# A grouped softmax streamed through one core: one broadcast multiply per tile in place of eight scalings, and tiles of 128 rows instead of 256

## The chip, the cores and the metric

The kernel runs on one core of a Trainium2 chip. A core has several engines that run side by side and meet only through semaphores. Four of them matter here. VectorE (DVE in the profile) reduces and does elementwise work. ScalarE (ACT) evaluates functions such as the exponential. SyncE (SP) has no arithmetic; it issues transfers. Sixteen DMA engines, shared by all, move data between the device memory (HBM) and the on-chip memory (SBUF), which has 128 partitions. The metric is the device time of one execution in microseconds (us); lower is better.

## The reference

The input is a tensor of 4 x 4096 rows of 4352 f32 numbers. Each row is cut into 8 groups of 544, and each group becomes a softmax of its own.

```python
def setup_inputs():
    B, N, D, G = 4, 4096, 4352, 8
    return {"x": np.random.randn(B, N, D).astype(np.float32)}

def reference(x):
    B, N, D = x.shape
    G = 8
    Dg = D // G
    x_g = x.reshape(B, N, G, Dg)
    x_g = x_g - x_g.max(axis=-1, keepdims=True)
    exp = np.exp(x_g)
    out = exp / exp.sum(axis=-1, keepdims=True)
    return out.reshape(B, N, D).astype(np.float32)
```

In all, 285 MB are read and 285 MB are written.

## The kernel before

The 16,384 rows are cut into 64 tiles of 256 rows. A tile puts two adjacent rows into each of the 128 partitions (`R = 2`), which makes 34,816 consecutive bytes per partition, in HBM as in SBUF. There are six buffers (`NBUF = 6`), and everything is done in place in a buffer: the tile is loaded into it, turned into exponentials, scaled, and stored from it.

A tile has two units of work, one for each of its two rows per partition. A unit is 128 rows, and it has two steps:

- `expo` (lines 55 to 69): VectorE takes the negated maximum of each of the 8 groups (line 58, one instruction over 128 x 4352 elements). ScalarE then does 8 activations (line 62), one for each group: each one takes exp(x - max) in place and sums its 544 results on the way. The profile shows each sum being read out as an instruction of its own.
- `scale` (lines 71 to 77): VectorE takes the reciprocals of the 8 sums (line 74), then does 8 multiplications (line 76), one for each group, each by one number per partition.

The order is written out by hand; no planner moves anything. Units are staggered by one: the loop emits `expo` of unit n and then `scale` of unit n-1. On VectorE this gives: maximum of unit n, reciprocals and scalings of unit n-1, maximum of unit n+1, and so on. ScalarE works on unit n while VectorE scales unit n-1.

All transfers are issued by SP on one queue, and the 16 DMA engines take them in the order of issue. At the start, `AHEAD = NBUF - 1`, so 5, loads are issued. After that, when the last unit of tile i has been scaled, SP issues the store of tile i (line 50) and then the load of tile i+5 (line 47). That load goes into the buffer of tile i-1, so it has to wait until the store of tile i-1 has landed. SP works strictly in order, so while a load waits there, the store of the next tile stands behind it.

Of the kernel before, what the change touches and what calls it, by code (L numbers as in the profile page):

```python
# [1 line left out]

# [4 lines left out]


@with_exitstack
def kernel(  # L10
    ctx: ExitStack,
    tc: tile.TileContext,
    x: bass.AP,
    out: bass.AP,
):
    nc = tc.nc
    G = 8
    P = 128
    R = 2
    NBUF = 6  # L20
    xf = x.flatten_outer_dims()
    of = out.flatten_outer_dims()
    N, D = xf.shape
    Dg = D // G
    f32 = mybir.dt.float32

    pool = ctx.enter_context(tc.tile_pool(name="io", bufs=NBUF))
    small = ctx.enter_context(tc.tile_pool(name="small", bufs=4))

    spans = []  # L30
    at = 0
    while at < N:
        r = min(R, (N - at) // P)
        spans.append((at, r))
        at += r * P
    nt = len(spans)
    tiles = {}
    sums = {}

    def rows(dram, i):  # L40
        at, r = spans[i]
        return dram[at:at + r * P].rearrange("(p r) d -> p (r d)", r=r)

    def load(i):
        xt = pool.tile([P, R * D], f32, name="xt")
        tiles[i] = xt
        nc.sync.dma_start(out=xt[:, :spans[i][1] * D], in_=rows(xf, i))  # L47

    def store(i):
        nc.sync.dma_start(out=rows(of, i), in_=tiles[i][:, :spans[i][1] * D])  # L50

    def row(i, r):
        return tiles[i][:, r * D:(r + 1) * D].rearrange("p (g d) -> p g d", g=G)

    def expo(i, r):
        xr = row(i, r)
        mx = small.tile([P, G], f32, name="mx")
        nc.vector.reduce_max(out=mx, in_=xr, axis=mybir.AxisListType.X, negate=True)  # L58
        sm = small.tile([P, G], f32, name="sm")
        sums[i, r] = sm  # L60
        for g in range(G):
            nc.scalar.activation(  # L62
                out=xr[:, g, :],
                in_=xr[:, g, :],
                func=mybir.ActivationFunctionType.Exp,
                bias=mx[:, g:g + 1],
                scale=1.0,
                accum_out=sm[:, g:g + 1],
            )

    def scale(i, r):
        xr = row(i, r)
        rs = small.tile([P, G], f32, name="rs")
        nc.vector.reciprocal(out=rs, in_=sums.pop((i, r)))  # L74
        for g in range(G):
            nc.vector.tensor_scalar_mul(  # L76
                out=xr[:, g, :], in0=xr[:, g, :], scalar1=rs[:, g:g + 1])

    AHEAD = NBUF - 1
    work = [(i, r) for i in range(nt) for r in range(spans[i][1])]
    with tc.manual_schedule():
        for i in range(AHEAD):
            load(i)
        for n in range(len(work) + 1):
            if n < len(work):
                expo(*work[n])
            if n:
                i, r = work[n - 1]  # L90
                scale(i, r)
                if r == spans[i][1] - 1:
                    store(i)
                    if i + AHEAD < nt:
                        load(i + AHEAD)


# [1 line left out]
_INS = ['x']  # L99
_OUTS = [((4, 4096, 4352), 'float32')]  # L100


# [23 lines left out]
```

## Time and profile before

| | |
|---|---|
| time, median of 3 runs | 1335.33 us (1334.61 to 1335.8) |
| profiled execution, its own time | 1335.33 us |
| span of that execution, first to last instruction | 1333.5 us |
| VectorE busy | 1041.7 us (78%), 1280 instructions |
| ScalarE busy | 764.4 us (57%), 2049 instructions |
| DMA engines busy with the kernel's queue | 99.3% of 16 engines' span |
| moved over the span | 428 GB/s, reads and writes together |

"Span" runs from the first to the last instruction of the profiled execution; what lies around it is in the execution's own time. A group of instructions is shown with its line in the kernel, its engine, its operation, what it writes and reads, how many there were, then busy time and mean duration in ns, and after the second bar the idle time of the engine just before these instructions with what ended most of it. "SPq" is SP's queue of DMA issues. For DMA issues the last number is the median time from issue to landing. Waiting of an engine that isn't the slowest costs nothing in itself.

### The profile page before, as it was taken

What the parts mean: (1) busy time and instruction counts of PE and PEld (TensorE: products, weight loads), DVE (VectorE), ACT (ScalarE), POOL (GpSimd) and SP (SyncE); (2) the same over time, 40 slices, a digit from 0 to 9 for tenths busy, and PEclk for the clock granted to TensorE, in tenths of its full rate; (3) what the DMA queues carried; (4) which work ended last, traced back from release to release, by engine and by line L of the source; (5) the groups of instructions that cost most, each with busy time, mean ns of one, the idle gap of its engine ahead of it and who ended that gap; (6) DMA issues with size and microseconds to landing.
All of it is one profiled execution on the core that took longest, in us unless ns stands there. A gap on an engine that the chain in (4) does not pass through costs nothing.

```text
span 1333.5 us, 3809 instructions
## 1 busy us (share of the span) xinstructions
DVE 1041.7 (78%) x1280; ACT 764.4 (57%) x2049; POOL 0.2 (0%) x4
## 2 busy tenths in 40 slices
DVE  5999887787877878778778787787877878778771
ACT  4777665555655556555565565655656556555560
POOL 0000000000000000000000000000000000000000
DMA  9999999999999999999999999999999999999996
GB/s 403 428 423 432 432 432 431 433 432 431 432 432 434 434 432 434 430 434 434 434 431 433 434 434 434 431 432 435 432 434 432 431 434 434 433 435 433 433 433 283
DMA packets 18460, 570.66 MB, mean 428 GB/s; under 512 B 2048, under 2 KB 2048, under 8 KB 2048
## 3 DMA queue, kind: packets, MB, share of 16 engines
q1 hardware_dynamic: 18432, 570.43, 99.3%
q14 instruction: 28, 0.23, 0.0%
HBM read 285.21 MB, written 285.21 MB: 428 GB/s over the span
## 4 chain that ended last, share of the span: by engine, by line
DMA 92%; DVE 4%; ACT 1%; SPq 1%; issue 0%; DVEq 0%; ACTq 0%
DMA out_dram<-xt 89%; DMA xt<-in_x_dram 3%; DVE mx L58 2%; DVE xt L76 1%; ACT xt L62 1%; SPq L47 1%; DVE rs L74 0%; DVEq L121 0%; ACTq L121 0%; ACTq L62 0%; SPq L50 0%
## 5 line engine op out<-in xcount | busy, mean ns | idle before, releaser
L62 ACT ACTIVATE xt<-xt,mx 128x544 f32<-128x544 f32 x1024 | 751.3, 735 | 522.0 <-DVE mx L58 504.4
L58 DVE TENSOR_REDUCE mx<-xt 128x8 f32<-128x4352 f32 x128 | 599.3, 4683 | 253.5 <-DMA xt<-in_x_dram 253.5
L76 DVE TENSOR_SCALAR xt<-xt,rs 128x544 f32<-128x544 f32 x1024 | 434.3, 499 | 4.5
L62 ACT ACTIVATION_READ_ACCUMULATOR xt<-xt,mx 128x1 f32 x1024 | 191.4, 187 | 0.0
L74 DVE RECIPROCAL rs<-sm 128x8 f32<-128x8 f32 x128 | 24.9, 194 | 4.0 <-ACT xt L62 4.0
L62 ACT ACT_TABLE_LOAD x1 | 1.3, 1283 | 13.7 <-DMA xt<-in_x_dram 13.7
L110 POOL MEMSET const-bfloat16-1.0<- 128x1 bf16 x1 | 0.1, 101 | 0.0
L110 POOL MEMSET const-uint8-127<- 128x1 uint8 x1 | 0.1, 101 | 0.0
L110 POOL MEMSET const-float32-0.0<- 128x1 f32 x1 | 0.1, 98 | 0.2 <-issue 0.2
L110 POOL MEMSET const-float32-1.0<- 128x1 f32 x1 | 0.1, 98 | 0.0
## 6 DMA issues: line engine op xcount, KB each, us to landing
xt<-in_x_dram SPq DMA_DIRECT2D x64, 4352.0 KB, 30.8
out_dram<-xt SPq DMA_DIRECT2D x64, 4352.0 KB, 40.7
```

What stands on the lines that cost most here:

```text
L47: nc.sync.dma_start(out=xt[:, :spans[i][1] * D], in_=rows(xf, i))
L58: nc.vector.reduce_max(out=mx, in_=xr, axis=mybir.AxisListType.X, negate=True)
L62: nc.scalar.activation(out=xr[:, g, :], in_=xr[:, g, :], func=mybir.ActivationFunctionType.Exp, bias=mx[:, g:g + 1], scale=1.0, accum_out= ...
L74: nc.vector.reciprocal(out=rs, in_=sums.pop((i, r)))
L76: nc.vector.tensor_scalar_mul(out=xr[:, g, :], in0=xr[:, g, :], scalar1=rs[:, g:g + 1])
L110: nc = _bacc.Bacc("TRN2", target_bir_lowering=False, num_devices=1)
```

## The change

Three things change together. A tile has 128 rows, one per partition (`R = 1`), so a transfer is half as large (17,408 bytes per partition), there are 128 tiles, and each tile is one unit of work. There are 12 buffers instead of 6; they take the same room. Loads run `NBUF - 2`, so 10, tiles ahead, and the load of tile i+10 goes into the buffer of tile i-2. And the 8 scalings of a unit become one multiplication of the 128 x 4352 unit by the reciprocals, in which each of the 8 numbers of a partition is repeated along its group by a step of zero.

```diff
@@ -16,8 +16,8 @@
     nc = tc.nc
     G = 8
     P = 128
-    R = 2
-    NBUF = 6
+    R = 1
+    NBUF = 12
...
@@ -72,13 +72,12 @@
         xr = row(i, r)
         rs = small.tile([P, G], f32, name="rs")
         nc.vector.reciprocal(out=rs, in_=sums.pop((i, r)))
-        for g in range(G):
-            nc.vector.tensor_scalar_mul(
-                out=xr[:, g, :], in0=xr[:, g, :], scalar1=rs[:, g:g + 1])
+        nc.vector.tensor_mul(
+            out=xr, in0=xr, in1=rs.unsqueeze(2).to_broadcast([P, G, Dg]))
...
-    AHEAD = NBUF - 1
+    AHEAD = NBUF - 2
```

## The prediction

> **What bounds the kernel now.** I read the page first, then the waits of the DMA-issuing queue, then that queue's issues in order of time, and last the stretches around the end. The page, parts 1, 3, 5 and 6:
>
> ```profile
> span 1333.5 us, 3809 instructions
> DVE 1041.7 (78%) x1280; ACT 764.4 (57%) x2049; POOL 0.2 (0%) x4
> ...
> q1 hardware_dynamic: 18432, 570.43, 99.3%
> ...
> L58 DVE TENSOR_REDUCE mx<-xt 128x8 f32<-128x4352 f32 x128 | 599.3, 4683 | 253.5 <-DMA xt<-in_x_dram 253.5
> L76 DVE TENSOR_SCALAR xt<-xt,rs 128x544 f32<-128x544 f32 x1024 | 434.3, 499 | 4.5
> ...
> L74 DVE RECIPROCAL rs<-sm 128x8 f32<-128x8 f32 x128 | 24.9, 194 | 4.0 <-ACT xt L62 4.0
> ...
> xt<-in_x_dram SPq DMA_DIRECT2D x64, 4352.0 KB, 30.8
> out_dram<-xt SPq DMA_DIRECT2D x64, 4352.0 KB, 40.7
> ```
>
> The 16 DMA engines work for 99.3% of the span. VectorE works for 78% and its largest idle time, 253.5 us, waits for a load. ScalarE waits for VectorE. So transfers set the pace. The queue that issues them waits too, for a buffer to be emptied:
>
> ```profile
> SPq L47 <- DMA out_dram<-xt: 1145.0, 58, 20.7
> ```
>
> That wait costs nothing while transfers are still queued. The issues near the end, in order of time, show the pace:
>
> ```profile
> 1167.27 0.33 SPq L47 DMA_DIRECT2D xt<-in_x_dram  x1
> ...
> 1188.74 0.33 SPq L47 DMA_DIRECT2D xt<-in_x_dram  x1
> ...
> 1209.31 0.33 SPq L47 DMA_DIRECT2D xt<-in_x_dram  x1
> ...
> 1229.89 0.33 SPq L47 DMA_DIRECT2D xt<-in_x_dram  x1
> ...
> 1250.45 0.33 SPq L47 DMA_DIRECT2D xt<-in_x_dram  x1
> ```
>
> A tile of 256 rows (one load and one store) takes 20.57 us, so a transfer takes 10.28; a load lands after 30.8, three transfers, a store after 40.7, four. Every sixth tile takes 0.9 us more (here 21.47). Last, the stretches at the end (busy time of VectorE, ScalarE and GpSimd, clock, DMA share, GB/s):
>
> ```profile
> 1305.00:1310.00 5.00, 0.00 (x0) 0.00 (x0) 0.00 (x0) 1.00 1.00 432
> ...
> 1320.00:1325.00 5.00, 0.00 (x0) 0.00 (x0) 0.00 (x0) 1.00 0.29 125
> 1325.00:1330.00 5.00, 0.00 (x0) 0.00 (x0) 0.00 (x0) 1.00 0.13 56
> ```
>
> Arithmetic is over by 1304 and the transfers still run at full rate for 15 us. Then most engines are done, and a share of 0.13 means that two of 16 go on to the end. The time is that of the slowest DMA engine, some 12 us behind the others.
>
> **The change part by part.** The profiled execution took 1335.33 us, 1.83 more than its span, and is itself the median of the three runs, so sums go straight against 1335.33.
>
> *VectorE.* Removed: 1024 scalings, 434.3 us. Added: 128 multiplies of 128x4352. The trace of before has no such instruction. Lower bound: the eight scalings as they stand, 3.39 us in a row. Upper bound: two operands read one after the other at the reduce's rate, 2 x 4.68 = 9.37. I take 4.68, the row of the reduce, which also goes once over 4352 f32 elements. That adds 128 x (4.68 - 3.39) = 165 us of VectorE work. A row's turn on VectorE is now 8.13 us (scalings start at 24.61, 32.74 and 40.87), of which 4.74 is not scaling; it becomes 4.74 + 4.68 = 9.42, while the transfers give a row 10.28. All 165 us lie beside transfers: cost 0. The cover ends at a multiply of 10.28 - 4.74 = 5.54 us; above it every 0.1 us costs 12.8.
>
> A rule speaks against this edit: the Trainium skill, "VectorE: DVE Perf Modes", section "The perf-mode tier table", has f32 tensor_scalar at two elements a cycle and tensor_tensor at one. The scaling row agrees with the first half (544 elements in 499 ns); no row here shows the second. Its section on the TRN2 errata gives (N+151)/0.96 ns for an f32 tensor_tensor, which for 4352 elements I estimate at 4.69 us: were VectorE the bound, +166 us; under the transfers, nothing.
>
> *Queue depth.* Loads go 10 tiles ahead in 12 buffers, so load i+10 waits for store i-2 instead of load i+5 for store i-1. When that store lands, four transfers of 5.14 us are still queued (loads i+8 and i+9, stores i-1 and i), 20.6 us; before, two of 10.28 (load i+4, store i), 20.6 too. What stands behind the waiting load on SP's queue is store i+1, and it is later than its data in both. In the steady part a tile's data lands 5.14 us after the landing on which I count, its row is scaled some 20 us later (its reduce 4.7, its exponentials 6.0, its turn behind the next reduce, the multiply), and the store's turn on SP comes seven tiles on, at 72 us. Nothing starves: cost 0.
>
> *Start.* The first load is half as long, so it lands near 8.5 us instead of 13.65, and store n is ready near 24 + 9.4n. SP first blocks at load 12, which waits for store 0, landing near 59; store 3 is ready at 52. The ten prefetched loads keep the engines busy to 54. An earlier start of arithmetic buys nothing, as DMA starts at 0.73 in both.
>
> *End.* The last load has five transfers to land (26 us) and its row needs some 20 more, but the last store comes to its turn behind about 13 transfers (67 us). The shorter last store is hidden as the longer one was: 0.
>
> *SP's issues.* 128 more at 0.33 to 0.46 us are some 50 us more on a queue that waited 1145: 0.
>
> *Transfers twice as many, half as long.* This is the part on the path. Each of 16 engines moves eight packets of 34,816 bytes per transfer now (16,384 in 128 transfers); it will move eight of 17,408 in each of 256. The trace's records of single packets, which no view lists, give 1,288 ns for 34,816 bytes and 309 ns for an instruction packet of 8,192. The difference, 979 ns for 26,624 bytes, is 36.77 ns per 1,000 bytes; eight packets at that rate are 10.24 us. The pace was 10.28. So about 0.04 us per transfer is not bytes (ends of packets, the semaphore write). 128 more of these: +5.0 us. Lower bound 0, if those 0.04 us are bytes after all. Upper bound: the same two records leave 1,288 - 1,280 = 8 ns per packet, 1,024 more packets per engine are 8.2, and 128 semaphore packets of 9 ns are 1.2: +9.4. I take 5.0, because the measured pace is shorter than eight whole records (10.30), so their ends overlap.
>
> The Trainium skill, "DMA: Bandwidth & Descriptors", section "Anatomy of one DMA", puts a fixed 2.0 us on each DMA: as a serial cost I estimate +256 us for 128 more. The pace speaks otherwise: 10.28 leaves room for 0.04, not 2, since further transfers stand queued.
>
> *Instruction fetches.* The packet records show an instruction packet ahead of each of the long tiles, about 124 us apart, on the engine that ends last; I read them as VectorE's, since six tiles are some 128 of its instructions. With 384 instead of 1280 compute instructions most of them go. But a second engine has its own, about 72 us apart (ScalarE's count fits), 0.62 us each, and ends only 0.4 us earlier. What is late next is therefore that one: -0.4 us, not -8.
>
> *Where loads and stores first meet.* Between 50 and 100 us the rate dips (page, second and third slice 428 and 423 against 433 later); smaller transfers could lengthen or shorten that, by less than 2 us either way: 0.
>
> Sum: 1335.33 + 5.0 - 0.4 = 1339.9.
>
> **The rivals.**
> 1. *Rate by bytes alone.* The 0.04 us is not per transfer: 1335 to 1337.9. For it: it is a difference of two near numbers, and the instruction packet goes to another memory. Against: a semaphore packet per engine and transfer is in the records.
> 2. *Faster: the fetch penalty shrinks with the packets.* A fetch takes 309 ns, but the data packet after it is also some 310 ns longer. If that second part follows the packet's size and falls away, ScalarE's 16 fetches cost 5 us less: 1335.33 - 0.4 - 5 + 5 = 1335 with my transfer cost, 1330 without it. It decides once the gain passes the transfer cost by 2.7. Nothing in the trace separates the two parts by size.
> 3. *Transfers get worse than their fixed cost.* Smaller pieces of memory turn by turn, with the packets of 1.4 to 2.2 us that the records show in the first 325 us lasting on. One more percent of the pace is 13 us: 1345 to 1360. Against: these packets vanish later on in before.
> 4. *VectorE becomes the bound.* A multiply over 5.54 us: at 6.0, 1335 + 59 = 1394; at 9.37, some 1825. Against: the reduce at 4.68 with the same element count.
>
> **How the numbers follow.** Forecast (1338.0 to 1344.5) 0.52; rate by bytes 0.25; faster 0.10; worse transfers 0.08; VectorE 0.05. The range 1333.5 to 1346 leaves out most of the faster case, most of the worse one and VectorE's, about 0.2. A measurement of this kernel tells 0.2%, 2.7 us, from no change: below 1332.7 faster, 0.10; between, 0.25; above 1338.0 slower, 0.65. The likeliest case's own range is 1338 to 1344.5.
>
> **What would show it.** Loads issued 10.32 us apart, not 10.28; DMA share still 99%; multiplies near 4.7 us and VectorE near 1225 us busy (599 + 25 + 128 x 4.69), 91% of the span; a load landing near 26 us and a store near 31; the rare long tiles at spacings that belong to ScalarE alone; the last engine again some 12 us behind. The prediction is wrong if a pace under 10.30 appears, if VectorE's idle time before the reduce goes to nothing, or if the engines end together.

## The result and the profile after

The changed kernel takes 1341.01 us (median of 4 runs, 1339.41 to 1341.88), the kernel before 1335.57 beside it (4 runs, 1334.61 to 1336.1). The ratio is 1.004, with a 95% interval of 1.0023 to 1.0058: slower by 0.4%. The forecast was 1339.9.

The profiled execution of the changed kernel took 1339.41 us, the least of its four; its span is 1337.6 against 1333.5. The lines of its page that answer to those of before:

```profile
span 1337.6 us, 3339 instructions
...
DVE 1210.8 (91%) x384; ACT 764.3 (57%) x2049; POOL 0.2 (0%) x4
...
q1 hardware_dynamic: 36864, 570.44, 99.6%
...
L58 DVE TENSOR_REDUCE mx<-xt 128x8 f32<-128x4352 f32 x128 | 599.6, 4684 | 83.7 <-DMA xt<-in_x_dram 83.7
L75 DVE TENSOR_TENSOR xt<-xt,rs 128x4352 f32<-128x4352 f32 x128 | 600.6, 4692 | 4.4
...
xt<-in_x_dram SPq DMA_DIRECT2D x128, 2176.0 KB, 25.8
out_dram<-xt SPq DMA_DIRECT2D x128, 2176.0 KB, 30.6
```

VectorE took on 169 us of work, and all of it came out of its idle time before the reduce (253.5 us before, 83.7 now). The transfers stayed the bound, at 99.6%. A load lands after five transfers, a store after six. The issues of SP's queue in the middle of the span show the pace, and one of the long tiles that remain (665.55 to 676.50):

```profile
634.57 0.33 SPq L47 DMA_DIRECT2D xt<-in_x_dram  x1
...
644.87 0.33 SPq L47 DMA_DIRECT2D xt<-in_x_dram  x1
...
655.25 0.33 SPq L47 DMA_DIRECT2D xt<-in_x_dram  x1
...
665.55 0.33 SPq L47 DMA_DIRECT2D xt<-in_x_dram  x1
...
676.50 0.33 SPq L47 DMA_DIRECT2D xt<-in_x_dram  x1
```

A tile of 128 rows takes 10.33 us (10.30, 10.38, 10.30), where half a tile of before took 10.28. Two stretches, as busy time of VectorE, ScalarE and GpSimd, clock, DMA share and GB/s, show the middle and the end. The kernel before:

```profile
600.00:900.00 300.00, 238.27 (x291) 172.92 (x464) 0.00 (x0) 1.00 1.00 433
```

The changed kernel:

```profile
600.00:900.00 300.00, 273.61 (x87) 172.90 (x464) 0.00 (x0) 1.00 1.01 431
...
1325.00:1330.00 5.00, 0.00 (x0) 0.00 (x0) 0.00 (x0) 1.00 0.31 132
1330.00:1335.00 5.00, 0.00 (x0) 0.00 (x0) 0.00 (x0) 1.00 0.09 38
```

The rate is down from 433 to 431 GB/s, and the end still belongs to one or two of the 16 DMA engines (a share of 0.09 is 1.4 of them).

A finer pace comes from the trace's records of landings, which no view lists: each transfer has 16, one per DMA engine. The first of the 16, followed from transfer to transfer over the last two thirds of the span, gives the pace of an engine that nothing disturbs; the distance from the first to the last is how late the last engine is. "Pace" and "lateness" below mean these two.

### The profile page after: what moved, and what is told of

It reads as the page before. It is cut to its first block, busy times and chain, and to the rows that moved or that the text cites. A ratio compares the mean times of both kernels' runs of the same rounds, so it can differ in the third digit from the quotient of the medians.

```text
span 1337.6 us, 3339 instructions
## 1 busy us (share of the span) xinstructions
DVE 1210.8 (91%) x384; ACT 764.3 (57%) x2049; POOL 0.2 (0%) x4
## 3 DMA queue, kind: packets, MB, share of 16 engines
q1 hardware_dynamic: 36864, 570.44, 99.6%
## 4 chain that ended last, share of the span: by engine, by line
DMA 83%; DVE 11%; issue 2%; ACT 1%; SPq 1%; ACTq 0%
DMA out_dram<-xt 80%; DVE xt L75 6%; DVE mx L58 5%; DMA xt<-in_x_dram 3%; ACT xt L62 1%; SPq L47 1%; DVE rs L74 0%; SPq L50 0%; ACTq L120 0%
## 5 line engine op out<-in xcount | busy, mean ns | idle before, releaser
L58 DVE TENSOR_REDUCE mx<-xt 128x8 f32<-128x4352 f32 x128 | 599.6, 4684 | 83.7 <-DMA xt<-in_x_dram 83.7
L75 DVE TENSOR_TENSOR xt<-xt,rs 128x4352 f32<-128x4352 f32 x128 | 600.6, 4692 | 4.4
```

What stands on the lines that cost most here:

```text
L75: nc.vector.tensor_mul(out=xr, in0=xr, in1=rs.unsqueeze(2).to_broadcast([P, G, Dg]))
```

## The experiments

Two accounts stood against each other at first: the transfers (twice as many, each with a fixed cost) and VectorE (165 us more work that is perhaps not quite covered).

### The multiply alone

```diff
 # kernel before, R = 2, NBUF = 6, AHEAD = 5
-        for g in range(G):
-            nc.vector.tensor_scalar_mul(...)
+        nc.vector.tensor_mul(
+            out=xr, in0=xr, in1=rs.unsqueeze(2).to_broadcast([P, G, Dg]))
```

> The kernel before with only the scalings replaced by the broadcast multiply; tiles stay at 256 rows. Transfer theory (the 5 us come from twice as many transfers, VectorE's extra work is covered): no slower than before, 1335.57 - 0.4 = about 1335, loads still 20.57 us apart, multiply 4.69 us, VectorE near 1210 us busy. VectorE theory (the longer multiply is what costs): about 1341, the time of the changed kernel.

Measured: 1335.49 us, ratio to before 0.9994 (0.9983 to 1.0005). The page of this kernel:

```profile
DVE 1207.3 (91%) x384; ACT 764.4 (57%) x2049; POOL 0.2 (0%) x4
```

VectorE is as busy as in the changed kernel, and nothing is lost against the 1335.75 of the kernel before beside it. The pace of the transfers is 10.283 us, that of before.

### The tiles alone

```diff
 # changed kernel, R = 1, NBUF = 12, AHEAD = 10
-        nc.vector.tensor_mul(...)
+        for g in range(G):
+            nc.vector.tensor_scalar_mul(
+                out=xr[:, g, :], in0=xr[:, g, :], scalar1=rs[:, g:g + 1])
```

> The changed kernel with the eight scalings put back; tiles of 128 rows, 12 buffers, 10 ahead. Transfer theory: as slow as the changed kernel, 1341, a little more (up to 0.7) if VectorE's fetches make its DMA engine the last again; pairs of transfers 10.33 us apart. VectorE theory: back to 1335.6.

Measured: 1341.78 us, ratio 1.0041 (1.0029 to 1.0053). VectorE is back to 1046.8 us (78%), and the loss is all there. With the run before, this settles it: the loss comes with the smaller transfers, and the multiply, in this place, costs nothing.

### More packets in as many transfers, and more transfers still

The first kernel keeps the 128 transfers but takes each partition's two rows from places 128 rows apart, so a partition's part is two pieces of 17,408 bytes:

```diff
 # kernel before; the tile's side of load and store is split in the same way
-        return dram[at:at + r * P].rearrange("(p r) d -> p (r d)", r=r)
+        return dram[at:at + r * P].rearrange("(r p) d -> p r d", r=r)
```

> The kernel before, but the two rows of a partition come from row p and row p+128 of the tile, so each partition's part is two pieces of 17,408 bytes: 128 transfers as before, twice the packets. If the cost sits with the packets: the pace of a transfer goes from 10.283 to near 10.32 and the time to 1339 to 1341. If it sits with the transfer (semaphore, issue): pace 10.283 and 1335.6.

The second cuts each transfer of the changed kernel into two halves of its columns:

```diff
 # changed kernel; store likewise
+        for h in range(0, D, D // 2):
+            nc.sync.dma_start(out=xt[:, h:h + D // 2], in_=rows(xf, i)[:, h:h + D // 2])
```

> The changed kernel with every transfer cut once more, into two of 8,704 bytes per partition: 512 transfers. Transfer theory, the measured 0.0436 us for each of 128 added ones, now 256 more: 1341 + 11 = 1352, DMA share still 99%. Rate by bytes alone (the 5 us came from something else in the change): 1341.

Measured: 1339.13 us (ratio 1.002, 1.0011 to 1.0029) and 1350.55 (1.0107, 1.0092 to 1.0122). The four kernels in order, per 4.456 MB (one transfer of before, or as many of the others as make that up):

| kernel | data packets per engine | semaphore packets per engine | pace, us |
|---|---|---|---|
| before | 8 | 1 | 10.283 |
| same transfers, split packets | 16 | 1 | 10.321 |
| changed kernel | 16 | 2 | 10.327 |
| half rows | 32 | 4 | 10.414 |

The first two differ by eight packets: 37.5 ns, 4.7 ns for each. The second and third differ by one semaphore packet: 6.1 ns. The fourth was not used for this, and these two sizes give it: 10.327 + 16 x 0.0047 + 2 x 0.0061 = 10.414. So, by the pace, the cost sits mostly with the packets and a little with the transfers. The medians say it more roughly: against the 1335.75 of the kernel before beside them, the split packets cost 3.4 us and the half rows 14.8, where 128 times the difference in pace is 4.8 and 16.7. What is left of 10.283 without them is 10.240 us, 435.2 GB/s.

The rate in the middle of the half-row kernel, in the same columns as above:

```profile
600.00:900.00 300.00, 270.93 (x86) 169.54 (x456) 0.00 (x0) 1.00 1.01 428
```

Its share stands at 1.01 and only 428 GB/s go through: engines that never rest and move less. The page of a kernel at a full DMA share doesn't show this cost as idle time; it shows it as GB/s.

### Larger transfers

```diff
 # kernel before, with the broadcast multiply
-    R = 2
-    NBUF = 6
+    R = 3
+    NBUF = 4
```

> The kernel before with tiles of 384 rows, three rows and 52,224 bytes per partition, 4 buffers, loads 3 ahead, and the broadcast multiply: 43 tiles, 86 transfers instead of 128. Transfer theory: 42 transfers fewer at 0.0436 us is 1.8 us less, and 0.4 less by VectorE's fetches, 1333.3. Against it: a start or an end that the larger tiles leave uncovered, 1336 or more.

Measured: 1340.14 us, ratio 1.0027 (1.0017 to 1.0038): slower, the case written against the theory. Its GB/s in 40 slices:

```profile
GB/s 414 361 400 441 430 428 436 430 427 441 428 434 431 430 434 438 430 436 431 430 445 425 430 443 427 437 436 428 436 435 430 439 430 430 445 425 436 438 388 338
```

The gain is there in the steady part: 15.403 us per transfer between 400 and 1200 us, and the sizes above give 1.5 x 10.240 + 8 x 0.0047 + 0.0061 = 15.403. But three loads of 15.4 us are used up before the first tile of three rows is ready, and the second and third slices drop to 361 and 400. In the records of landings 8.0 us are lost by 100 us, against 1.4 in the kernel before: 6.6 more, which the 1.8 gained don't pay for. A cover that the smaller tiles have is gone at the start.

### The last engine: fewer instructions, and more

To test what makes the last engine late, one kernel takes the maximum and its subtraction out of the computation, and with them most instructions:

```diff
 # kernel before, with the broadcast multiply
-        nc.vector.reduce_max(out=mx, in_=xr, axis=mybir.AxisListType.X, negate=True)
-        for g in range(G):
-            nc.scalar.activation(... bias=mx[:, g:g + 1], accum_out=sm[:, g:g + 1])
+        nc.scalar.activation(out=xr, in_=xr, func=mybir.ActivationFunctionType.Exp)
...
+        nc.vector.reduce_sum(out=sm, in_=xr, axis=mybir.AxisListType.X)
```

> The kernel before without the maximum and its subtraction (left out of the computation): one activation over a whole row of 8 groups, then the sums by VectorE, the reciprocals and the broadcast multiply. Same transfers, ScalarE 128 activations instead of 1024 with 1024 reads. Fetch theory: nearly no fetches, the last engine's 12 us shrink to 2 or 3, about 1326. If the lateness of the last engine has another cause: 1335.

Measured: 1329.12 us, ratio 0.9949 (0.9937 to 0.996). Its page, and the end:

```profile
DVE 1218.4 (92%) x384; ACT 484.4 (36%) x129; POOL 0.2 (0%) x4
...
q14 instruction: 6, 0.05, 0.0%
```

```profile
1320.00:1325.00 5.00, 0.00 (x0) 0.00 (x0) 0.00 (x0) 1.00 0.23 97
1325.00:1330.00 5.00, 0.00 (x0) 0.00 (x0) 0.00 (x0) 1.00 0.01 3
```

The packets of the kind "instruction" are what is called fetches here. With 6 of them in place of 28, the pace is 10.283, that of before, and the lateness at the end is 6.0 us instead of 12.2. So half of the lateness is left nearly without fetches; the expectation of 2 or 3 us was too small. The landing records of the kernel before show the other half directly: up to 330 us the lateness comes to 6.0, and from there to 12.3 it rises in seven steps of 0.94 to 1.02 us, each 4 to 7 us after an instruction packet of the series that stands some 124 us apart. What makes the 6 us that fetches don't explain (3.2 of them are there by 140 us in this run) stays open.

Sixteen tiny activations more per row were to double ScalarE's fetches:

```diff
 # kernel before, after the 8 activations of a row
+        for k in range(16):
+            nc.scalar.activation(
+                out=junk[:, :1], in_=mx[:, :1],
+                func=mybir.ActivationFunctionType.Exp, bias=mx[:, 0:1], scale=1.0)
```

> The kernel before with 16 tiny activations of one column more in each row's work on ScalarE, results unused: ScalarE's instructions nearly double, its work stays under the pace of the transfers. Fetch theory (the last DMA engine is late by instruction fetches, 0.62 us each): 16 more fetches, about 10 us more, 1345, and the stretch with few engines at the end about 22 us long. If fetches don't set the end: 1335.6.

Measured: 1431.54 us, ratio 1.0713 (1.07 to 1.0727). This says nothing on fetches:

```profile
DVE 1048.2 (73%) x1280; ACT 1338.9 (94%) x4097; POOL 0.2 (0%) x4
...
L72 ACT ACTIVATE junk<-mx 128x1 f32<-128x1 f32 x2048 | 600.7, 293 | 62.6
```

An activation of one column takes 293 ns, and ScalarE became the bound. With 8 instead of 16 it does not:

```diff
-        for k in range(16):
+        for k in range(8):
```

> As the run with 16 extra activations in each row, but 8: that run made ScalarE the bound (94% busy, 293 ns each), so it said nothing on fetches. With 8, a row takes ScalarE 6.0 + 8 x 0.32 = 8.6 us, under the 10.28 of the transfers. Fetch theory: half as many ScalarE instructions again, 8 fetches more at 0.62 us, about 5 us more, 1340 to 1341, the last engine some 17 us behind. If fetches don't set the end: 1335.7.

Measured: 1341.1 us, ratio 1.0046 (1.0023 to 1.0068). The median is 4.5 us over the 1336.62 of the kernel before beside it, near the 5 expected. But the 12 executions spread from 1338.77 to 1355.26, which also lifts the ratio, and the profile shows the slowest of them, to which the next section returns.

### How deep the queue must be

Loads one tile further ahead, in the changed kernel:

```diff
-    AHEAD = NBUF - 2
+    AHEAD = NBUF - 1
```

> The changed kernel with loads 11 ahead instead of 10: load i+11 waits for store i-1, so only two transfers of 5.16 us are queued when that store lands. Slowest-engine theory: the last engine always has work, time stays 1341, while the others can lead it by no more than about 10 us, so they end closer together. If the choice of 10 ahead matters for the time: several us more.

Measured: 1372.14 us (1360.12 to 1377.6), ratio 1.0257 (1.0224 to 1.0289). The expectation was plainly wrong. Stretches of this kernel:

```profile
400.00:600.00 200.00, 188.56 (x61) 118.77 (x319) 0.00 (x0) 1.00 1.01 431
600.00:650.00 50.00, 45.68 (x16) 28.04 (x77) 0.00 (x0) 1.00 1.01 432
650.00:700.00 50.00, 42.63 (x14) 29.73 (x80) 0.00 (x0) 1.00 1.00 417
700.00:750.00 50.00, 43.40 (x15) 24.27 (x65) 0.00 (x0) 1.00 1.00 391
```

Up to 650 us it runs like the changed kernel; then the rate breaks. In the landing records the lateness has just grown to 6.9 us there, and it is 7.8 one tile on. A load now waits for the store issued just before it, and that store counts as landed only when the last engine is through. On the last engine two transfers (10.3 us) are then still queued, and on the others less by the lateness.

How much the quickest engine still has to do when a load is issued can be read from the records: it is the time from the issue of that load to the first landing of the transfer ahead of it. Call it the lead. What the load loses is the step from that landing to its own first landing, less the pace. For the loads between 300 and 1250 us, in this run and in the profiled execution with 8 extra activations:

| lead, us | 11 ahead: loads, mean loss in us | 8 extra activations: loads, mean loss in us |
|---|---|---|
| 2.7 or more | 53, 0.0 | 36, 0.0 |
| 2.1 to 2.7 | 24, 0.5 | 3, 0.4 |
| under 2.1 | 12, 1.2 | 5, 1.4 |

Under a lead of some 2.7 us a load comes late by about what is missing, in both runs. In the profiled executions of the kernel before and of the changed kernel the lead never fell under 9 us. Arithmetic has little to do with it: stores waited for VectorE's multiply only twice in the whole run.

```profile
SPq L50 <- DVE xt L75: 9.9, 2, 5.0
```

The packet records don't show the engines idle meanwhile. The share stays at 1.00, and the lost time stands in longer packets: between 700 and 750 us 163 are over 0.1 us above their usual 0.648 us, against 1 between 600 and 650. Why it shows as longer packets was not tried.

If lateness against depth is the cause, a kernel with little lateness must stand 11 ahead:

```diff
 # the kernel without the maximum
-    R = 2
-    NBUF = 6
+    R = 1
+    NBUF = 12     # AHEAD = NBUF - 1 = 11
```

> The run without the maximum (left out of the computation, as are its subtraction and most of ScalarE's instructions) with tiles of 128 rows, 12 buffers and loads 11 ahead. Theory that the run 11 ahead collapsed because the last engine's lateness outgrew the two transfers still queued: here the lateness stays near 6 us, so no collapse, 1329.1 + 5.6 = about 1335. If 11 ahead is bad in itself (a wait of SP on the store just issued): some 30 us more, 1360.

Measured: 1332.93 us, ratio to before 0.9967 (0.9956 to 0.9978), a lateness of 6.0 us at the end, a lead that never fell under 4.1 us between 300 and 1250 us, and no break:

```profile
600.00:900.00 300.00, 279.22 (x90) 111.06 (x29) 0.00 (x0) 1.00 1.01 431
900.00:1200.00 300.00, 276.96 (x86) 111.06 (x29) 0.00 (x0) 1.00 1.01 432
```

It is slower than the same kernel with large tiles, whose ratio to before was 0.9949 and whose span is 1327.3 against 1331.8 here: the price of the packets once more.

The same account explains the spread with 8 extra activations. In that profiled execution the lateness came to 18.1 us by 990 us and to 20.0 by 1044, near the 20.6 that are queued there; the lead fell under 2.7, and the rate broke:

```profile
600.00:900.00 300.00, 234.38 (x286) 231.44 (x682) 0.00 (x0) 1.00 1.00 434
900.00:1050.00 150.00, 115.39 (x145) 115.53 (x341) 0.00 (x0) 1.00 1.00 427
1050.00:1200.00 150.00, 113.16 (x139) 113.30 (x335) 0.00 (x0) 1.00 1.00 412
```

With loads 4 ahead, 41 us are queued:

```diff
 # the kernel with 8 extra activations
-    AHEAD = NBUF - 1
+    AHEAD = NBUF - 2
```

> The run with 8 extra activations per row, with loads 4 ahead instead of 5, so that 41 us of transfers stand queued instead of 20.6. There the last engine fell up to 18.9 us behind and single executions rose to 1355. Theory that the rise comes from lateness outgrowing the queue: no execution above 1345, full rate up to the end, median 1339 to 1341 (the fetches alone, 5 us over 1336), last engine 17 to 20 us behind. If the rise has another cause: the same wide spread as before, some executions from 1347 to 1355.

Measured: 1341.02 us, 4.7 over the 1336.34 of the kernel before beside it, ratio 1.0026 (1.0005 to 1.0048), seven executions within 1340.05 to 1343.02, and the same stretches at full rate:

```profile
900.00:1050.00 150.00, 117.31 (x141) 115.26 (x340) 0.00 (x0) 1.00 1.00 433
1050.00:1200.00 150.00, 118.50 (x150) 117.33 (x345) 0.00 (x0) 1.00 1.00 433
```

The lateness reached 17.2 us and did no harm beyond itself.

The kernel before, with the same step:

```diff
-    AHEAD = NBUF - 1
+    AHEAD = NBUF - 2
```

> The kernel before with loads 4 ahead instead of 5: load i+4 waits for store i-2, so four transfers of 10.28 us, 41 us, are queued when that store lands, instead of 20.6. Theory that depth beyond the last engine's lateness (12 us) buys nothing: 1335.7, same pace. If more depth helps, so that the changed kernel's choice was worth something on its own: 1 to 3 us less.

Measured: 1336.84 us, ratio 1.0002 (0.9991 to 1.0013). In the kernel before, depth beyond the lateness buys nothing that can be told.

No version found computes all of the reference and beats the kernel before by more than can be told. The two faster ones leave out the maximum, which on inputs far from zero guards the exponential against overflow.

## Why the prediction was right

The forecast, +4.6 us, had the sign, the cause and nearly the size of the measured +5.4. By its own steps, on the two profiled executions (whose last landings lie 4.25 us apart, 1332.57 and 1336.82):

| term | predicted, us | shown, us |
|---|---|---|
| VectorE's 165 us more | 0 | 0 (multiply alone: 1335.49, beside 1335.75) |
| queue depth, start, end, SP's issues | 0 | +0.1 in the first landing; the rest not visible |
| twice as many transfers | +5.0 | 128 x (2 x 5.1635 - 10.2834) = +5.6 |
| instruction fetches | -0.4 | -0.7 (lateness 12.2 to 11.5) |
| where loads and stores first meet | 0, under 2 either way | -0.8 (1.4 to 0.6 us lost before the steady pace) |

- *VectorE.* The reduce's row was the right stand-in: 4.68 taken, 4.692 measured, and VectorE at 91%. The upper bound of 9.37 was far off. (The busy time of 1225 us was the sum of the three rows, which came out; the page's 1210.8 is lower because instructions overlap a little.) The Trainium skill, "VectorE: DVE Perf Modes", in its section on the TRN2 errata, gives (N+151)/0.96 ns for an f32 tensor_tensor, from which 4.69 us had been estimated; the row of 4692 ns agrees. The broadcast form does cost VectorE more than the eight scalings, 4.69 us against 3.39, and the time did not move, because VectorE was not the bound. That the scalings' row agrees with two elements a cycle was read too freely: eight of them in 3.39 us are 1.28 elements a ns, against 0.93 in the reduce, more but not twice as many.
- *Transfers.* The 0.04 us per transfer, taken as a small difference between two packet records and the pace, is 0.0436. It was put down to "ends of packets, the semaphore write" together; the runs split it: eight packets of 4.7 ns and one semaphore packet of 6.1. The Trainium skill, "DMA: Bandwidth & Descriptors", section "Why small descriptors are slow (HBM only)", puts about 3 cycles on each packet; at the 850 MHz of its section "Where 436 GB/s comes from" I estimate 3.5 ns. The runs' 4.7 ns is a third more. The page warns of this for pieces of 256 bytes; here it is most of a loss of 0.4% at 17,408. The Trainium skill's section "Anatomy of one DMA", from which the prediction took 2.0 us for each DMA, is about transfers issued by GpSimd. SP issues all of these, and 128 more of them cost 5.6 us by the pace, not 256.
- *Fetches.* That an engine late by ScalarE's fetches would be the next last one was right: the 0.7 us gained are far from the 8 that the vanishing fetches of VectorE alone suggest, and the long tiles left over stand 73 us apart (603.62 to 676.50), ScalarE's spacing. The 0.7 itself compares one execution with one, and the lateness varies: the multiply alone, with the same fetches gone, ended at 10.3. What the step did not see is that fetches make only half of the lateness.
- *Queue depth and start.* The first load landed at about 10 us and not at 8.5, and the load said to block first went out at 62.92 and not near 59; neither shows in the time. The depth was costed at nothing, with the cover named: 20.6 us in both. That cover is needed, as the run 11 ahead shows, 31 us slower than the changed kernel. The prediction gave the depth as equal and did not ask how much of it the last engine's 12 us use up.
- The 1.3 us between the difference of the profiled executions (4.1) and that of the medians (5.4) is mostly that the profiled execution of the changed kernel was its fastest of four.
- *Luck.* The mechanism was right, but a hit within 1.1 us is partly luck. The +5.0 rests on a difference of 979 ns between two records given to whole ns; one ns more or less there moves the term by 1.3 us. On the profiled executions its shortfall of 0.6 and the 0.8 that was costed at nothing nearly cancel.

Of the rivals, the rate by bytes alone is out (half rows: +15 us on before). The faster case, a fetch penalty that shrinks with the packets, is out too: the long tiles of the changed kernel are 0.62 us over the others (10.95 against 10.33), the size that ScalarE's fetches had with the larger packets. The packet records say the same: the packet behind such a fetch is 0.28 us over its usual 0.648 us in the changed kernel, and 0.31 to 0.36 over 1.288 before. VectorE as the bound and lasting long packets did not show.

## What to carry to other kernels

Where DMA engines are full, look at GB/s and not at the busy share: packets have a fixed price (4.7 ns here), and more work on another engine is free as long as its turn stays under the transfers' pace (9.4 us under 10.3 here). Read the end of the span for how late the last DMA engine is, and keep more transfers queued, at the moment the awaited store lands, than that lateness and some 3 us to spare; below that the rate breaks, which here cost far more than the packets. Large tiles save packets only until the first one comes too late for the prefetched loads to cover it.

## What was not expected of the hardware

- The rate without packet costs, 435.2 GB/s, is the same for pieces of 8,704 to 52,224 bytes, for loads and stores in turn. The section "Where 436 GB/s comes from" of the Trainium skill's "DMA: Bandwidth & Descriptors" has 435.2 GB/s as the ceiling of the ports, and the runs agree to the digit; its limit of some 358 GB/s for memory does not bind in this kernel on one core, where 433 were sustained.
- DMA engines that share one queue drift apart, here by 12 us in 1330, and the quicker ones don't wait for the last as long as transfers stand queued. Instruction packets, 0.2 MB of 570, make half of it: each takes 309 ns and delays its engine by 0.6 to 0.9 us, since the data packet after it is 0.3 to 0.6 us longer too.
- The break of the rate when the drift nearly uses up the queue's depth: from 432 to 391 GB/s within 100 us, once the quickest engine has less than some 2.7 us of work left when the next load is issued.
